# A decoder on one core: where the last norm's weights are scaled, when the low part of the summed squares is multiplied, and in which order normed blocks are read

## The chip, the core and the metric

The kernel runs on one core of a Trainium2 chip. Its engines each work off a queue of their own: TensorE (PE in the profile, its weight loads PEld), VectorE (DVE), ScalarE (ACT), GpSimd (POOL) and SyncE (SP), which here issues transfers. An instruction starts when those ahead of it on its engine have started and the semaphores that it waits for have come. The metric is the device time of one execution in microseconds (us), the median of the runs.

## What is computed

The reference is a decoder of two layers on 512 tokens of 1024 features in float32. Each layer is a half-step feed-forward block, a mixer (gated linear attention in layer 0, stick-breaking attention in layer 1) and a second half-step feed-forward block; a norm stands ahead of each, and one at the end.

```python
def rmsnorm(x, g):
    xf = x.astype(jnp.float32)
    y = xf * lax.rsqrt(jnp.mean(xf * xf, axis=-1, keepdims=True) + EPS)
    return (y * g.astype(jnp.float32)).astype(x.dtype)

def swiglu(h, w_gate, w_up, w_down):
    return (jax.nn.silu(h @ w_gate) * (h @ w_up)) @ w_down

for i in range(DEPTH):
    x = x + 0.5 * swiglu(rmsnorm(x, ffn1_norm[i]), ffn1_w_gate[i], ffn1_w_up[i], ffn1_w_down[i])
    h = rmsnorm(x, mix_norm[i])
    y = gla_mixer(h, ...) if i % N_MIXERS == 0 else sb_mixer(h, ...)
    x = x + y
    x = x + 0.5 * swiglu(rmsnorm(x, ffn2_norm[i]), ffn2_w_gate[i], ffn2_w_up[i], ffn2_w_down[i])
return rmsnorm(x, final_norm)
```

## The kernel before

**Layout.** x is kept feature by feature: eight blocks xs[k] of 128 features by 512 tokens. A product in float32 accuracy is three products of rounded parts: each matrix is split into a high part (a cast on ScalarE) and a low part (the matrix less its high part, on VectorE), and TensorE adds high by high, low by high and high by low (`mm3`). Weights are wh and wl (`Entry.parts`, cast L151, low part L152), with four buffers each. The rows of the profile name a product by its result and the two factors: ps_f<-nh,wl is a product into ps_f.

**Order of the work.** Work for TensorE stands in a list of entries (`Feed`); an entry is a stretch of weight columns with a body that yields after each quarter. Starting an entry also starts the loads and splits of the next ones. A planner then lays out each engine's queue from this program: it takes what is ready by its own estimates, and of that what comes first in the program. `tc.issue_after(ins)` adds an edge that keeps an instruction behind ins in the queue of the engine on which ins runs; `tc.high_priority` moves an instruction forward.

**A feed-forward stage** (`FFN.run`; four of them, at about 20, 553, 875 and 1430 us) goes like this. Its first entries (`feat`) multiply blocks that are not normed yet, only scaled by the gain (xh, xl), and the result is scaled by the norm's factor R afterwards; so TensorE needn't wait for the norm. `two_halves` runs the first two entries (a gate and an up column block) side by side, in halves of twelve products: gate, up, gate, up. After the third of these, in three of the stages, `sums_wide` puts in the sum over features: the squares, added up in ss by ScalarE and VectorE, are split into sh (cast, L605) and sl (low part, L607), and two products with a matrix of ones, ps_R<-sh and ps_R<-sl, give each token's sum on all partitions. Both stand behind `recent[-4]`, the fourth last product traced so far, so ahead of the last block's three products of that gate entry. `rstd_wide` makes R of it: v on VectorE (L617), logarithm, exponential and square on ScalarE (through L653), two more operations on VectorE (L624, L625).

**Normed blocks.** While entries three to six run, `normed_input` makes the normed blocks in four pieces, a pair each: piece j scales blocks j and j + 4 (xn, L878), splits both (nh L884, nl L885) and takes four differences of halves (ts, L894), from which later products are made. Entries seven and eight (numbers 6 and 7 counted from 0, still `feat`) read these blocks instead of the raw ones: `st["h"], st["l"]` are then nh and nl. All `feat` entries read the blocks in the order 0 to 7. Later column blocks (`seven`, L776) use products of halves, seven in place of eight, with weights that are sums too (s), their gates and ups in tiles o; `down` entries multiply back (ps_d, L80) and add to x: VectorE's update (L365), or for some blocks ScalarE's scaling and an adding transfer that GpSimd issues (L360, L361).

**The end.** In the last stage `to_tokens` runs between the `down` entries and the last product. It loads the final gain onto all partitions (fin, a transfer that GpSimd issues, L1636), transposes x to tokens on TensorE (L1641), copies the result on ScalarE (L1646), and scales fin on VectorE (L1649). The scaling is traced inside `tc.issue_after(copied)`, where copied is the last of the copies on ScalarE. `back_tok` does the last product by tokens (ps_bt), and `last` adds it to x (L1656), takes the final norm and sends the rows out (L1669 to L1684).

Of the kernel before, what the change touches and what calls it, by code (L numbers as in the profile page):

```python
# [21 lines left out]
KD = D // P  # L22
# [8 lines left out]
def turns(t):  # L31

    return t.rearrange("p (two n) -> p n two", two=2)


def flat(ps):

    return ps.rearrange("p (n two) -> p two n", two=2)


def pair(t):

    return t.rearrange("p (two n) -> p two n", two=2)
# [3 lines left out]
def decoder(ctx: ExitStack, tc: tile.TileContext, a: dict, out: bass.AP):  # L47
    nc = tc.nc
# [12 lines left out]
    def psum(name, tag=None):  # L61
        if tag is None:
            tag = order[turn_[0] % 8]
            turn_[0] += 1
        return pp.tile([P, T], F32, tag=tag, bufs=banks[tag], name=name)
# [9 lines left out]
    ones_r = one_r.to_broadcast([P, P])  # L75
# [3 lines left out]
    def mm(ps, l, r, first, last):  # L79
        st["pe"] = nc.tensor.matmul(ps, l, r, start=first, stop=last).ins  # L80
        recent.append(st["pe"])

    recent = []

    def mm3(ps, wh, wl, mh, ml, first, last):
        mm(ps, wh, turns(mh), first, False)
        mm(ps, wl, turns(mh), False, False)
        mm(ps, wh, turns(ml), False, last)
# [128 lines left out]
    def feat(ch, f, evac, tag=None, defer=None):  # L217


        def body(W):  # L220
            (wh, wl), = W
            ps = psum("ps_f", tag)
            for part in (range(u, u + KD // 4) for u in range(0, KD, KD // 4)):
                for k in part:
                    mm3(ps, wh[:, k], wl[:, k], st["h"][k], st["l"][k], k == 0, k == KD - 1)
                if part[-1] == KD - 1:
                    if defer is None:
                        evac(ps)
                    else:
                        defer.append((evac, ps))  # L230
                yield

        feed.q.append(Entry([(ch, lambda t: t[:, :, f * P : (f + 1) * P], KD, P)], body))
        feed.q[-1].evac = evac
# [97 lines left out]
    def down(w, r0, nf, hs, part, nxt, late=0, homes=()):  # L332


        nd = KD // nf
        src = w[r0 : r0 + nf * P, part * nd * P : (part + 1) * nd * P]
        ch = Chunk(src.rearrange("(f p) c -> p f c", p=P), nf, nd * P)
        ch.few = True

        def body(W):  # L340
            (wh, wl), = W
            acc = []

            def prod(m, fs):
                if m == len(acc):
                    acc.append(psum("ps_d"))
                s = slice(m * P, (m + 1) * P)
                for f in fs:
                    mm3(acc[m], wh[:, f, s], wl[:, f, s], hs[f][0], hs[f][1], f == 0, f == nf - 1)

            if late:
                for m in range(nd):
                    prod(m, range(nf - late))
            for m in range(nd):
                prod(m, range(nf - late if late else 0, nf))
                ps = acc[m]
                k = part * nd + m
                if m < len(homes):
                    d = sp.tile([P, T], F32, tag=homes[m], name="d")
                    nc.scalar.activation(pair(d), flat(ps), AF.Copy, scale=0.5)  # L360
                    nc.gpsimd.dma_start(xs[k], d, accum_op=ALU.add)  # L361
                    yield
                    continue
                x = pair(xs[k])
                nc.vector.scalar_tensor_tensor(  # L365
                    out=x, in0=flat(ps), scalar=0.5, in1=x, op0=ALU.mult, op1=ALU.add
                )
                if nxt is not None:
                    nxt(k)
                yield  # L370

        feed.q.append(Entry([(ch, lambda t: t, nf, nd * P)], body))
# [151 lines left out]
    st = {}  # L524
# [76 lines left out]
    def sums_wide(pool, after):  # L601

        ss = st["ss"]
        h = sp.tile([P, T], F32R, tag="sq", name="sh")
        nc.scalar.copy(h, ss)  # L605
        l = pool.tile([P, T], F32R, tag="t", name="sl")
        nc.vector.tensor_tensor(out=l, in0=ss, in1=h.bitcast(F32), op=ALU.subtract)  # L607
        st["wide"] = ps = psum("ps_R")
        with tc.high_priority(100), tc.issue_after(after):
            mm(ps, ones_r, turns(h), True, False)  # L610
            mm(ps, ones_r, turns(l), False, True)

    def rstd_wide():

        ps = st["wide"]
        v = sp.tile([P, T], F32, tag="ss", name="v")
        nc.vector.tensor_scalar(  # L617
            out=pair(v), in0=flat(ps), scalar1=1.0 / D, scalar2=EPS, op0=ALU.mult, op1=ALU.add
        )
        y = st["R"] = sp.tile([P, T], F32, tag="sq", name="R")  # L620
        act(y, v, AF.Ln)
        act(y, y, AF.Exp, scale=-0.5)
        nc.scalar.activation(ps, y, AF.Square)
        nc.vector.scalar_tensor_tensor(out=v, in0=ps, scalar=-0.5, in1=v, op0=ALU.mult, op1=ALU.mult)  # L624
        nc.vector.scalar_tensor_tensor(out=y, in0=v, scalar=1.5, in1=y, op0=ALU.add, op1=ALU.mult)  # L625

    def two_halves(between=None):

        feed.finish()
        g = [feed.start(), feed.start()]  # L630
        for i in range(3):
            for n, x in enumerate(g):
                next(x, None)
                next(x, None)
                if between is not None and (i, n) == (1, 0):
                    between(recent[-4])

    def new_norm():
        st["h"], st["l"] = st["nh"], st["nl"]

    def flush(deferred):
        for evac, ps in deferred:
# [3 lines left out]
    def exp_ln_tables(after):  # L646
        with tc.issue_after(after):
            st["tab"] = nc.scalar.preload_act_table_set("natural_log_exp_and_others").ins
# [7 lines left out]
    class FFN:  # L656
# [328 lines left out]
        def run(self, between=None):  # L985
            with tc.tile_pool(name="hp", bufs=8, reuse_waits="tile") as self.hp, tc.tile_pool(
                name="tp", bufs=5, reuse_waits="tile"
            ) as self.tp:
                st["few"] = self.hp
                new_norm()  # L990
                if st["ss"] is not None:
                    if self.after_ffn:
                        exp_ln_tables(st["closed"])
                    two_halves(lambda after: sums_wide(self.tp, after))
                    rstd_wide()
                flush(self.defer)
                def spread(todo, n):
                    for i in range(n):
                        for piece in todo[i * len(todo) // n : (i + 1) * len(todo) // n]:
                            with behind(self.last_up):  # L1000
                                piece()
                        feed.entries(1)

                spread(self.normed_input(), self.NORMED - 2)
                self.normed = True
                st["h"], st["l"] = zip(*self.n)
                todo = self.sums()
                spread(todo[:5], self.sums_by - self.NORMED)
                feed.entries(1, True)
                for piece in todo[5:]:  # L1010
                    piece()
                feed.entries(self.count - self.sums_by - 1, True)
                if between is not None:
                    with tc.issue_after(st["closed"]):
                        nc.scalar.preload_act_table_set("sqrt_and_others")
                    feed.q[feed.pos].split()
                    between(self.tp)
                feed.entries(self.total - self.count)
# [612 lines left out]
    xt = {}  # L1631

    def to_tokens(tp):
        st["tp"] = tp
        fin = st["fin"] = tp.tile([P, D], F32, tag="s", bufs=4, name="fin")
        nc.gpsimd.dma_start(fin, a["final_norm"].partition_broadcast(P))  # L1636
        for hf in range(2):
            ps = [psum("ps_T") for _ in range(NT)]
            for m in range(4):
                for i in range(NT):  # L1640
                    nc.tensor.transpose(  # L1641
                        ps[i][:, m * P : (m + 1) * P], xs[hf * 4 + m][:, i * P : (i + 1) * P], ident
                    )
            for i in range(NT):
                xt[i, hf] = xs[hf * 4 + i]
                copied = nc.scalar.copy(xt[i, hf], ps[i]).ins  # L1646

        with tc.issue_after(copied):
            nc.vector.tensor_scalar(out=fin, in0=fin, scalar1=2.0 * float(D) ** 0.5, scalar2=None, op0=ALU.mult)  # L1649

    def last(dh, i, ps, c0, c1):
# [336 lines left out]
```

## Time and profile before

| | us |
|---|---|
| median of 3 runs | 1767.38 |
| lowest, highest | 1766.87, 1767.44 |
| the profiled execution | 1767.14 |
| its span, first to last instruction | 1765.2 |
| mean granted TensorE clock | 0.999 |

The profile is of one execution. Its page gives busy times by engine. A list of waits has one line for an engine and code line and what it waited for: us in total, times, longest. A timeline row has the start, the length, the engine, the line, the operation, out<-in and the shapes, and in brackets how long the engine had idled before it and what ended that. Times are from the span's start. The ends of TensorE's products are modelled, so rows of TensorE overlap. A row of windows has the window, its length, and the busy time with the count of instructions for PE, PEld, DVE, ACT and POOL, then clock and transfer rates.

### The profile page before, as it was taken

The page shows a single profiled execution, that of the slowest core. Times are in us where ns is not written, and L with a number is a line of the kernel's source. Part 1 is how long each engine was busy: PE and PEld are TensorE (multiplying, and loading weights), DVE is VectorE, ACT ScalarE, POOL GpSimd, SP SyncE. Part 2 cuts the span into 40 slices and gives each one's busy share as a digit, 9 for nine tenths or more (in the row PEclk, how much of TensorE's full clock was granted, in tenths as well). Part 3 has the DMA queues.
Part 4 walks back from the last instruction along what each step waited for, and adds up shares of the span by engine and source line. Part 5 has one row for each costly group of instructions (what it writes and reads, how often), then busy time and mean ns, then how long its engine had stood idle before and what let it go on. Part 6 is the DMA issues. An engine that isn't in the chain of part 4 may idle for free.

```text
span 1765.2 us, 31380 instructions
## 1 busy us (share of the span) xinstructions
PE 1751.6 (99%) x12714; PEld 1630.2 (92%) x12714; DVE 1506.7 (85%) x2490; ACT 1063.3 (60%) x1899; POOL 55.7 (3%) x77
## 2 busy tenths in 40 slices
PE   9999999999999999999999999999999999999998
PEld 8999999889888899999989999999888889999997
DVE  8999797786888999889799988977898679997986
ACT  7556555554655565555656555656888745555555
POOL 0000000200000000000000000010000000000000
PEclk9999999999999999999999999999999999999999
DMA  5543435422123433444434334352212234434341
GB/s 168 155 122 106 136 105 149 113 72 72 50 89 103 125 114 120 120 120 126 133 94 132 106 123 135 102 131 83 84 49 74 70 96 132 132 99 129 110 136 61
DMA packets 186389, 193.14 MB, mean 109 GB/s; under 512 B 4931, under 2 KB 171125, under 8 KB 186245
## 3 DMA queue, kind: packets, MB, share of 16 engines
q1 hardware_dynamic: 177760, 175.91, 31.9%
q0 software_dynamic: 8240, 14.95, 4.6%
q8 instruction: 99, 1.62, 0.4%
q14 instruction: 46, 0.37, 0.1%
q10 hardware_dynamic: 244, 0.29, 0.0%
HBM read 175.17 MB, written 2.10 MB: 100 GB/s over the span
## 4 chain that ended last, share of the span: by engine, by line
PE 86%; DVE 9%; ACT 3%; issue 1%; DMA 1%; SPq 0%; DVEq 0%; ACTq 0%
PE ps_w L776 22%; PE ps_d L80 15%; PE ps_q L776 11%; PE ps_f L80 10%; PE ps_z L776 5%; PE ps_w L410 5%; PE ps_t L80 4%; PE ps_b L80 3%; PE ps_q L410 2%; DVE wl L152 1%; PE ps_z L410 1%; PE ps_z L1476 1%; PE ps_oT L1561 1%; DVE xn L878 1%; PE ps_bt L80 1%
## 5 line engine op out<-in xcount | busy, mean ns | idle before, releaser
L152 DVE TENSOR_TENSOR wl<-raw,wh 128x1024 fp32r<-128x1024 f32 x241 | 255.1, 1059 | 40.7 <-ACT wh L151 40.0
L151 ACT CAST wh<-raw 128x1024 fp32r<-128x1024 f32 x241 | 222.2, 923 | 71.5 <-PE ps_f L80 25.4
L152 DVE TENSOR_TENSOR wl<-s,wh 128x1024 fp32r<-128x1024 f32 x160 | 195.2, 1220 | 64.5 <-ACT wh L151 64.0
L776 PE MATMUL ps_w<-th,wh 128*128 128x256 f32 x864 | 239.0, 277 | 0.2
L776 PE MATMUL ps_w<-th,wl 128*128 128x256 f32 x864 | 237.7, 275 | 1.2 <-DVE wl L152 1.2
L776 PE MATMUL ps_w<-tl,wh 128*128 128x256 f32 x864 | 237.6, 275 | 0.0
L151 ACT CAST wh<-s 128x1024 fp32r<-128x1024 f32 x160 | 168.6, 1054 | 6.0 <-DVE s L762 6.0
L776 PEld LDWEIGHTS ps_w<-th,wh 128*128 128x128 f32 x864 | 165.8, 192 | 1.4 <-ACT o L813 1.1
L776 PEld LDWEIGHTS ps_w<-th,wl 128*128 128x128 f32 x864 | 165.8, 192 | 1.4 <-DVE wl L152 1.4
L80 PE MATMUL ps_f<-xh,wh 128*128 128x512 f32 x432 | 166.4, 386 | 0.0
L776 PEld LDWEIGHTS ps_w<-tl,wh 128*128 128x128 f32 x864 | 165.9, 192 | 0.0
L80 PE MATMUL ps_f<-xh,wl 128*128 128x512 f32 x432 | 164.2, 380 | 0.5 <-DVE wl L152 0.5
L80 PE MATMUL ps_f<-xl,wh 128*128 128x512 f32 x432 | 163.9, 379 | 0.0
L80 PE MATMUL ps_d<-hh,wh 128*128 128x512 f32 x416 | 157.8, 379 | 0.0
L80 PE MATMUL ps_d<-hh,wl 128*128 128x512 f32 x416 | 157.7, 379 | 0.0
L80 PE MATMUL ps_d<-hl,wh 128*128 128x512 f32 x416 | 157.7, 379 | 0.0
L152 DVE TENSOR_TENSOR wl<-rawd,wh 128x1024 fp32r<-128x1024 f32 (+1 forms) x100 | 94.8, 961 | 8.0 <-ACT wh L151 8.0
L804 ACT COPY ps_z<-ps_w 128x256 f32<-128x256 f32 x72 | 26.0, 362 | 118.1 <-PE ps_w L776 117.9
L361 POOL DMA_DIRECT2D x<-d x53 | 46.0, 913 | 1555.0 <-ACT d L360 1097.4
L80 PEld LDWEIGHTS ps_f<-xl,wh 128*128 128x128 f32 x432 | 81.7, 189 | 11.6
L80 PEld LDWEIGHTS ps_f<-xh,wl 128*128 128x128 f32 x432 | 81.7, 189 | 11.4 <-DVE wl L152 0.9
L80 PEld LDWEIGHTS ps_f<-xh,wh 128*128 128x128 f32 x432 | 81.7, 189 | 10.8
(357 smaller groups left out, 5426.0 us busy)
## 6 DMA issues: line engine op xcount, KB each, us to landing
raw<-in_ffn_w_gate_dram SPq DMA_DIRECT2D x43, 1024.0 KB, 5.4
raw<-in_ffn_w_up_dram SPq DMA_DIRECT2D x43, 1024.0 KB, 5.4
rawd<-in_ffn_w_down_dram SPq DMA_DIRECT2D x84, 512.0 KB, 3.9
x<-d POOLq DMA_DIRECT2D x53, 256.0 KB, 4.6
raw<-in_gla_w_in_dram SPq DMA_DIRECT2D x12, 1024.0 KB, 5.3
raw<-in_sb_w_in_dram SPq DMA_DIRECT2D x16, 512.0 KB, 3.7
raw<-in_gla_w_out_dram SPq DMA_DIRECT2D x4, 1024.0 KB, 5.6
raw<-in_sb_w_in_dram SPq DMA_DIRECT2D x4, 1024.0 KB, 5.1
```

The costliest lines, as they stand in the source:

```text
L80: st["pe"] = nc.tensor.matmul(ps, l, r, start=first, stop=last).ins
L151: nc.scalar.copy(h[:, k], part)
L152: nc.vector.tensor_tensor(out=l[:, k], in0=part, in1=h[:, k].bitcast(F32), op=ALU.subtract)
L361: nc.gpsimd.dma_start(xs[k], d, accum_op=ALU.add)
L410: st["pe"] = nc.tensor.matmul(ps, l_, r_, start=first and c + n == 0, stop=c == 1 and n == 2, skip_group_check=True).ins
L776: st["pe"] = nc.tensor.matmul(o, l_, r_, start=first and j + n == 0, stop=j == 3 and n == 2, skip_group_check=True).ins
L804: v["copied"] = nc.scalar.copy(z, w).ins
L878: nc.vector.scalar_tensor_tensor(out=t, in0=xs[k], scalar=g, in1=st["R"], op0=ALU.mult, op1=ALU.mult)
L1476: nc.tensor.matmul(o_, l_, r_, start=first, stop=last, skip_group_check=True)
L1561: nc.tensor.matmul(po[e * 64 : e * 64 + 64, j * P : T], self.v[j][:, c : c + 64], self.wt[p, e][bk][:, c0 : c0 + n], start=j == 0, stop=j ...
```

## The change

Three edits. `feat` reads the blocks in the order of `st["made"]`: 0 to 7 for raw blocks (set in `new_norm`), and 0, 4, 1, 5, 2, 6, 3, 7 once the blocks are normed. In `sums_wide` the product with sl stands behind `recent[-1]`, the last product traced, and no longer right behind the one with sh. The scaling of fin stands behind VectorE's last update of x (`st["updated"]`, set in `down`) instead of the last copy on ScalarE.

```diff
@@ feat
-                for k in part:
-                    mm3(ps, wh[:, k], wl[:, k], st["h"][k], st["l"][k], k == 0, k == KD - 1)
+                for i in part:
+                    k = st["made"][i]
+                    mm3(ps, wh[:, k], wl[:, k], st["h"][k], st["l"][k], i == 0, i == KD - 1)
@@ down
-                nc.vector.scalar_tensor_tensor(
+                st["updated"] = nc.vector.scalar_tensor_tensor(
                     out=x, in0=flat(ps), scalar=0.5, in1=x, op0=ALU.mult, op1=ALU.add
-                )
+                ).ins
@@ sums_wide
-        with tc.high_priority(100), tc.issue_after(after):
-            mm(ps, ones_r, turns(h), True, False)
-            mm(ps, ones_r, turns(l), False, True)
+        for r, ins, first in ((h, after[0], True), (l, after[1], False)):
+            with tc.high_priority(100), tc.issue_after(ins):
+                mm(ps, ones_r, turns(r), first, not first)
@@ two_halves
-                    between(recent[-4])
+                    between((recent[-4], recent[-1]))
@@ new_norm
-        st["h"], st["l"] = st["nh"], st["nl"]
+        st["h"], st["l"], st["made"] = st["nh"], st["nl"], range(KD)
@@ FFN.run
                 st["h"], st["l"] = zip(*self.n)
+                st["made"] = [k for j in range(4) for k in (j, j + 4)]
@@ to_tokens
-                copied = nc.scalar.copy(xt[i, hf], ps[i]).ins
-
-        with tc.issue_after(copied):
+                nc.scalar.copy(xt[i, hf], ps[i])
+
+        with tc.issue_after(st["updated"]):
             nc.vector.tensor_scalar(out=fin, in0=fin, scalar1=2.0 * float(D) ** 0.5, scalar2=None, op0=ALU.mult)
```

## The prediction

> **What bounds the kernel now.** I read the page first, then the waits of TensorE alone, then stretches of the timeline around each place that the change touches.
>
> ```profile
> span 1765.2 us, 31380 instructions
> ...
> PE 1751.6 (99%) x12714; PEld 1630.2 (92%) x12714; DVE 1506.7 (85%) x2490; ACT 1063.3 (60%) x1899; POOL 55.7 (3%) x77
> ```
>
> TensorE is busy for 99% of the span: the time is its queue of products, and only what shortens that queue, or a wait inside it, moves the end. The change removes no product, so it can win waits alone. TensorE's waits name two of them:
>
> ```profile
> PE ps_w L776 <- DVE wl L152: 1.2, 1, 1.2
> ...
> PE ps_f L80 <- DVE nl L885: 0.8, 3, 0.3
> ```
>
> These columns say too little. A product of 512 columns is drawn 0.38 long, yet in an undisturbed run the next one starts 0.22 after it (0.11 for 256 columns). So I price a wait by start to start against that spacing, and I count the product behind the wait too, which comes about 0.10 late.
>
> **First part: the last norm's weights.** These rows are of VectorE, ScalarE and TensorE near the end.
>
> ```profile
> 1713.49 0.69 DVE L1649 TENSOR_SCALAR fin<-fin 128x1024 f32<-128x1024 f32 x1 [4.02 <-DMA fin<-in_final_norm_dram]
> 1714.10 1.22 DVE L152 TENSOR_TENSOR wl<-s,wh 128x1024 fp32r<-128x1024 f32 x1
> ...
> 1735.29 1.23 DVE L152 TENSOR_TENSOR wl<-raw,wh 128x1024 fp32r<-128x1024 f32 x1 [0.30 <-ACT wh L151]
> ...
> 1740.30 0.69 DVE L1656 SCALAR_TENSOR_TENSOR x<-ps_bt,x 128x512 f32<-128x512 f32 x1 [3.78 <-PE ps_bt L80]
> ...
> 1710.38 1.05 ACT L151 CAST wh<-s 128x1024 fp32r<-128x1024 f32 x1
> ...
> 1713.82 0.28 PE L776 MATMUL ps_z<-nl,wh 128*128 128x256 f32 x1
> 1713.93 0.28 PE L776 MATMUL ps_w<-th,wh 128*128 128x256 f32 x1
> 1715.37 0.38 PE L776 MATMUL ps_w<-th,wl 128*128 128x256 f32 x1 [1.16 <-DVE wl L152]
> 1715.58 0.28 PE L776 MATMUL ps_w<-tl,wh 128*128 128x256 f32 x1
> ```
>
> The scaling of fin stands in VectorE's queue from 1709.5 (1713.49 less 4.02) and waits for its DMA. So the old edge to a copy on ScalarE holds back nothing on VectorE. Behind it is the low part of a weight (L152), whose cast was done at 1710.38 + 1.05 = 1711.43, and TensorE waits for that low part. Start to start the wait takes 1715.37 - 1713.93 - 0.11 = 1.33, and the product behind it 0.21 - 0.11 = 0.10: **1.43 in all**. Without the scaling ahead of it the low part runs from about 1711.5 to 1712.7, 1.2 before TensorE asks for it at 1713.93 + 0.11, so the whole of it is won. No DMA moves, and POOL and SP issue what they issued.
>
> The scaling's new place is behind the last update of x, just ahead of or behind the low part at 1735.29. It holds VectorE for 0.61 (1713.49 to 1714.10). Queued behind it are that low part, which belongs to the last weights of the final product, and the update at 1740.30, before which VectorE idles for 3.78; that idle time hides it. With this cover gone it would cost 0.61. The weights landed long before.
>
> **Second part: the summed squares.** Three stages begin with them; the rows are of the first, the second and the third.
>
> ```profile
> 560.06 0.48 PE L80 MATMUL ps_R<-sh,one_r 128*128 128x512 f32 x1
> 560.79 0.48 PE L80 MATMUL ps_R<-sl,one_r 128*128 128x512 f32 x1 [0.24 <-DVE sl L607]
> 561.11 0.38 PE L80 MATMUL ps_f<-xh,wh 128*128 128x512 f32 x1
> ...
> 561.54 0.38 PE L80 MATMUL ps_f<-xl,wh 128*128 128x512 f32 x1
> ...
> 561.31 0.69 DVE L617 TENSOR_SCALAR v<-ps_R 128x512 f32<-128x512 f32 x1 [0.57 <-PE ps_R L80]
> ...
> 561.95 1.05 ACT L151 CAST wh<-raw 128x1024 fp32r<-128x1024 f32 x1 [1.94 <-PE ps_f L80]
> 562.90 0.63 ACT L653 ACTIVATE R<-v 128x512 f32<-128x512 f32 x1
> ...
> 882.51 0.38 PE L80 MATMUL ps_R<-sh,one_r 128*128 128x512 f32 x1
> ...
> 882.94 0.38 PE L80 MATMUL ps_f<-xh,wh 128*128 128x512 f32 x1
> ...
> 883.79 1.05 ACT L151 CAST wh<-raw 128x1024 fp32r<-128x1024 f32 x1 [2.41 <-PE ps_f L80]
> 884.74 0.62 ACT L653 ACTIVATE R<-v 128x512 f32<-128x512 f32 x1
> ...
> 1437.73 0.38 PE L80 MATMUL ps_R<-sh,one_r 128*128 128x512 f32 x1
> ...
> 1438.55 0.38 PE L80 MATMUL ps_f<-xh,wh 128*128 128x512 f32 x1
> ```
>
> In the first, the two products of the sums take 561.11 - 560.06 = 1.05. The first of them was late itself, so the product behind it keeps its 0.32; with the low part no longer waited for the two take 0.32 + 0.22 = 0.54: **0.51 won**. Moved behind three products it starts near 561.04, after the 560.79 at which its input was there. In the third, 0.82 becomes 0.44: **0.38**. In the second, 882.94 - 882.51 = 0.43 shows no wait: nothing.
>
> What is late next? VectorE's v (L617) waits for the low part, ScalarE's logarithm (L653) for v, and all normed blocks for that. But the logarithm also stands behind the weight cast, which waits for the three products that now come earlier. In the first stage their last one moves from 561.54 to 560.82, so cast and logarithm move from 561.95 and 562.90 to 561.23 and 562.18; v, from 561.45 to 562.14, is just in time. VectorE's chain is then 0.72 earlier. In the second the cast comes at 883.57 and the logarithm at 884.52: 0.22 earlier.
>
> **Third part: the order of the normed blocks.** Rows of the fifth to eighth product entry of a stage, then of the very first stage.
>
> ```profile
> 587.24 0.38 PE L80 MATMUL ps_f<-nh,wl 128*128 128x512 f32 x1
> 587.87 0.48 PE L80 MATMUL ps_f<-nl,wh 128*128 128x512 f32 x1 [0.25 <-DVE nl L885]
> 588.19 0.38 PE L80 MATMUL ps_f<-nh,wh 128*128 128x512 f32 x1
> ...
> 588.41 0.68 DVE L885 TENSOR_TENSOR nl<-xn,nh 128x512 fp32r<-128x512 f32 x1
> ...
> 589.35 1.22 DVE L152 TENSOR_TENSOR wl<-raw,wh 128x1024 fp32r<-128x1024 f32 x1
> ...
> 591.00 0.38 PE L80 MATMUL ps_f<-nh,wl 128*128 128x512 f32 x1
> ...
> 911.18 1.22 DVE L152 TENSOR_TENSOR wl<-raw,wh 128x1024 fp32r<-128x1024 f32 x1
> ...
> 912.84 0.38 PE L80 MATMUL ps_f<-nh,wl 128*128 128x512 f32 x1
> ...
> 44.81 0.90 PE L80 MATMUL ps_f<-nh,wh 128*128 128x512 f32 x2
> ...
> 45.76 0.38 PE L80 MATMUL ps_d<-hh,wh 128*128 128x512 f32 x1
> ...
> 46.49 0.38 PE L80 MATMUL ps_f<-nh,wh 128*128 128x512 f32 x1
> ...
> 47.65 1.22 DVE L152 TENSOR_TENSOR wl<-raw,wh 128x1024 fp32r<-128x1024 f32 x1
> 49.08 0.38 PE L80 MATMUL ps_f<-nh,wl 128*128 128x512 f32 x1
> ...
> 24.10:48.80 24.70, 24.12 (x108) 19.87 (x108) 24.70 (x44) 15.64 (x25) 0.00 (x0) 1.00 0.17 53
> ```
>
> Blocks are made in pairs 0 and 4, 1 and 5, 2 and 6, 3 and 7, and read from 0 to 7; block 3, of the last pair, is read fourth and waited for. That is 587.87 - 587.24 - 0.22 = 0.41, and 0.10 behind it: 0.51, in three stages (the waits list counts three): **1.53**. In the new order it is read seventh, nine products or 1.9 later. The last block's low part ends at 588.41 + 0.68 = 589.09 and is read two products ahead of 591.00, less what TensorE has won (1.02): 589.5, in time.
>
> The wait that could take its place is the next entry's weight: its low part ends at 589.35 + 1.22 = 590.57, is seen about 0.06 later, and is wanted at 591.00. TensorE will be there 0.51 + 0.51 = 1.02 sooner (589.98), the weight 0.72 sooner (589.91): just in time by 0.07. In the second stage 912.84 - 0.51 = 912.33 stands against 911.18 + 1.22 + 0.06 - 0.22 = 912.24. I take no cost; the bound on the other side, with VectorE not earlier at all, is 0.65 + 0.10, 0.13 + 0.10, and for the third (0.89 won there against the same 0.37 to spare) 0.52 + 0.10: 1.6.
>
> In the first stage the same waits cost 0.90 - 0.60 = 0.30 and 46.49 - 45.76 - 0.43 = 0.30. There VectorE is busy for all of 24.70 us before 48.80 (third time of the last row) and has no reason to be earlier. Its next low part ends at 47.65 + 1.22 = 48.87, and TensorE takes it at 49.08, so TensorE would now wait there for what it has won. I take 0; the bounds are 0.60 won and 0.15 lost (a new wait's 0.10 and rounding).
>
> **Sum.** 1.43 + 0.51 + 0.38 + 1.53 = 3.85 us. The profiled execution took 1767.14 with a span of 1765.2, and becomes 1763.3; it lies 0.24 under the median of the runs, so for the median 1767.38 - 3.85 = **1763.5**.
>
> The Trainium skill, TensorE: Matmul & The Clock Gate, section Single matmul latency, gives a lone warm matmul (398 + N) / 2.4 ns, 379 for 512 columns, while a stream is spaced by about 216: a wait then costs its idle time and 163 ns, and nothing is said of the product behind. The rows have the 0.38 and the 0.22. By the page the 0.10 behind each of six waits would not be there to win, and the sum would be about 3.25.
>
> **Rivals.**
> - *VectorE doesn't come earlier*, and the next weight's low part takes the place of the wait for block 3 in all three stages: 1763.5 + 1.6 = 1765.1. For it: the 0.07 to spare. Against it: the cast's release, worked out above.
> - *The first stage keeps what it wins*: 1763.5 - 0.6 = 1762.9. For it: the program that orders the queues may place other products in the gap, as it did with the ps_d at 45.76. Against it: VectorE's full queue.
> - *The 0.10 behind the waits isn't won*: 1763.5 + 0.6 = 1764.1. Against it: every wait above shows it. The page named above would give this.
> - *The first part doesn't do what it says*: the planner puts another wait into that place, and TensorE's 1.43 stays: 1764.9. Against it: nothing else stands in VectorE's idle 4.02.
> - *Slower*: one low part of a weight falls back in VectorE's queue. The planner orders by its own estimates, and these move. If the split at 589.35 falls behind two other splits (1.22 each) and a low part of a block (0.68), TensorE waits 3.12 - 0.07 + 0.10 = 3.15 in each of the three stages, 9.45 in all: 1773.0. It decides from 1.3 a stage on, where it eats the 3.85. Against it: in that stretch VectorE works off its queue in the order of the program, which the change leaves.
>
> **Chances.** The sum as it stands 0.57 (its own range 1763.0 to 1763.8); the first stage keeps its gain 0.13; VectorE not earlier 0.14; the 0.10 stays 0.04; the first part fails 0.05; slower 0.07. About 0.2% (3.5 us, to 1763.85) is what a measurement can tell from no change; so faster is 0.57 + 0.13 = 0.70, within it 0.14 + 0.04 + 0.05 = 0.23, slower 0.07. The sum lies only 0.3 beyond that bound. The range goes from 1762.9 less 0.6 (the spread of the runs) to 1763.5 + 1.6 + 1.43, two rivals at once: 1762.3 to 1766.5, with only the slower case outside.
>
> **What would show it.** Right: no wait for fin on VectorE, its scaling near 1734; no wait for sl; no wait for nl; starts 0.22 apart from 587 to 590. Wrong: a wait of TensorE for wl at the eighth entry, near 590, 912 or 1467, of more than 0.1; a wait in the first stage near 48 that is much shorter or longer than 0.5; VectorE's logarithm chain not earlier; or a different order on VectorE between 565 and 596. The forecast as a whole fails if new waits of 3 us or more appear in stages that the change doesn't touch.

## The result, and the profile after

The changed kernel takes 1763.96 us in the median of 17 runs (1763.23 to 1765.51), the kernel before 1767.44 in 17 runs beside it (1766.87 to 1769.01). The ratio is 0.9979 with a 95% interval of 0.9972 to 0.9985: 3.48 us, or 0.2%, are won. The prediction was 1763.5, a sum of 3.85 us. The interval of the ratio, 2.65 to 4.95 us, holds that too; what is missing of it is read from the traces.

First the head of the page after, then a line of the list of TensorE's waits:

```profile
span 1762.0 us, 31383 instructions
...
PE 1750.1 (99%) x12714; PEld 1630.7 (93%) x12714; DVE 1506.8 (86%) x2490; ACT 1064.1 (60%) x1899; POOL 55.6 (3%) x77
```

```profile
PE ps_f L80 <- DVE wl L152: 1.0, 2, 0.5
```

The engines' counts are those of before: only waits went. The list no longer has a line for nl, for sl or for the 1.2 of ps_w. In its place the one line on ps_f and wl has grown: before it counted one wait of 0.5, now two. The new one stands in the first stage, below. (Code lines are one or two higher than before.)

**The end.** Timeline of the changed kernel, VectorE and then TensorE:

```profile
1709.67 1.23 DVE L152 TENSOR_TENSOR wl<-s,wh 128x1024 fp32r<-128x1024 f32 x1 [2.00 <-ACT wh L151]
...
1731.69 0.68 DVE L1651 TENSOR_SCALAR fin<-fin 128x1024 f32<-128x1024 f32 x1
...
1737.08 0.69 DVE L1658 SCALAR_TENSOR_TENSOR x<-ps_bt,x 128x512 f32<-128x512 f32 x1 [3.57 <-PE ps_bt L80]
...
1712.14 0.28 PE L777 MATMUL ps_w<-th,wh 128*128 128x256 f32 x1
1712.25 0.28 PE L777 MATMUL ps_w<-th,wl 128*128 128x256 f32 x1
1712.36 0.28 PE L777 MATMUL ps_w<-tl,wh 128*128 128x256 f32 x1
```

The low part now waits for its own cast only, ends at 1709.67 + 1.23 = 1710.90, and TensorE reads it 1.35 later. The three products start 0.11 apart, where 1.33 and 0.10 were lost. The scaling of fin runs at 1731.69, and VectorE still idles for 3.57 (3.78 before) ahead of its next update.

**The sums.** The first of the three stages, a weight load (PEld), TensorE and ScalarE, and behind them the product with sh and the logarithm of the second:

```profile
560.27 0.18 PEld L80 LDWEIGHTS ps_R<-sh,one_r 128*128 128x128 f32 x1
...
560.39 0.38 PE L80 MATMUL ps_R<-sh,one_r 128*128 128x512 f32 x1
560.61 0.38 PE L80 MATMUL ps_f<-xh,wh 128*128 128x512 f32 x1
...
561.04 0.38 PE L80 MATMUL ps_f<-xl,wh 128*128 128x512 f32 x1
561.25 0.38 PE L80 MATMUL ps_R<-sl,one_r 128*128 128x512 f32 x1
...
562.46 0.64 ACT L654 ACTIVATE R<-v 128x512 f32<-128x512 f32 x1
...
881.80 0.38 PE L80 MATMUL ps_R<-sh,one_r 128*128 128x512 f32 x1
...
883.86 0.64 ACT L654 ACTIVATE R<-v 128x512 f32<-128x512 f32 x1
```

Both products of the sums stand in the stream at its spacing, and so do those of the other two stages. Even the product with sh, 0.13 late before, is on time here, though its load came only 0.12 ahead of it; the last section returns to that. From the product with sh to the logarithm it is 562.46 - 560.39 = 2.07, and was 562.90 - 560.06 = 2.84: 0.77 shorter. In the second stage it is 2.06 against 884.74 - 882.51 = 2.23: 0.17 shorter.

**The normed blocks.** The same stage up to its eighth entry, VectorE, weight loads and TensorE, then the same two products in the two stages that follow:

```profile
588.91 1.22 DVE L152 TENSOR_TENSOR wl<-raw,wh 128x1024 fp32r<-128x1024 f32 x1
...
589.75 0.19 PEld L80 LDWEIGHTS ps_f<-nh,wh 128*128 128x128 f32 x1
590.18 0.19 PEld L80 LDWEIGHTS ps_f<-nh,wl 128*128 128x128 f32 x1 [0.25 <-DVE wl L152]
...
589.96 0.38 PE L80 MATMUL ps_f<-nh,wh 128*128 128x512 f32 x1
590.18 0.48 PE L80 MATMUL ps_f<-nh,wl 128*128 128x512 f32 x1
590.50 0.38 PE L80 MATMUL ps_f<-nl,wh 128*128 128x512 f32 x1
...
911.60 0.48 PE L80 MATMUL ps_f<-nh,wl 128*128 128x512 f32 x1
911.91 0.38 PE L80 MATMUL ps_f<-nl,wh 128*128 128x512 f32 x1
...
1466.46 0.48 PE L80 MATMUL ps_f<-nh,wl 128*128 128x512 f32 x1
1466.78 0.38 PE L80 MATMUL ps_f<-nl,wh 128*128 128x512 f32 x1
```

No product waits for nl. But look at the loads. The one at 589.75 belongs to the product at 589.96: in the stream a load stands one product ahead of the product that uses it. The low part of the weight ends at 588.91 + 1.22 = 590.13, and its load comes at 590.18, together with its product and not ahead of it. That product isn't late (590.18 - 589.96 = 0.22); it is only drawn 0.48 long. The next one is late: 590.50 - 590.18 - 0.22 = 0.10. The same 0.10 stands at 1466.78 and, with its rounding, at 911.91.

**The first stage**, VectorE and TensorE:

```profile
47.89 1.22 DVE L152 TENSOR_TENSOR wl<-raw,wh 128x1024 fp32r<-128x1024 f32 x1
...
43.55 0.38 PE L80 MATMUL ps_f<-nl,wh 128*128 128x512 f32 x1
...
48.30 0.38 PE L80 MATMUL ps_f<-nh,wh 128*128 128x512 f32 x1
49.16 0.48 PE L80 MATMUL ps_f<-nh,wl 128*128 128x512 f32 x1 [0.49 <-DVE wl L152]
49.48 0.38 PE L80 MATMUL ps_f<-nl,wh 128*128 128x512 f32 x1
...
86.03 0.38 PE L777 MATMUL ps_w<-th,wh 128*128 128x256 f32 x1
```

A wait of 49.16 - 48.30 - 0.22 = 0.64, and 0.10 behind it, have taken the place of two waits of 0.30: about 0.15 lost.

### The profile page after: what moved, and what is told of

Same layout as the page of the kernel before. It is cut to its first block, busy times and chain, and to the rows that moved or that the text cites. A ratio compares the mean times of both kernels' runs of the same rounds, so it can differ in the third digit from the quotient of the medians.

```text
span 1762.0 us, 31383 instructions
## 1 busy us (share of the span) xinstructions
PE 1750.1 (99%) x12714; PEld 1630.7 (93%) x12714; DVE 1506.8 (86%) x2490; ACT 1064.1 (60%) x1899; POOL 55.6 (3%) x77
## 4 chain that ended last, share of the span: by engine, by line
PE 88%; DVE 7%; ACT 3%; issue 1%; DMA 1%; SPq 0%; DVEq 0%; ACTq 0%
PE ps_w L777 20%; PE ps_d L80 15%; PE ps_f L80 14%; PE ps_q L777 10%; PE ps_z L777 5%; PE ps_w L411 5%; PE ps_t L80 4%; PE ps_b L80 4%; PE ps_q L411 2%; DVE wl L152 2%; PE ps_z L1478 1%; PE ps_z L411 1%; PE ps_oT L1563 1%; PE ps_bt L80 1%; PE ps_T L1548 1%
```

## The experiments

The theory after these readings: the waits are won as they were priced, and the eighth entry's weight takes back 0.10 in each of three stages and 0.15 in the first. The rivals: a part doesn't work by itself for the reason given, or the losses are chance of one execution. Effects of 0.1 to 0.5 us are below the spread of the runs, so they are read from start to start in the traces, with the medians beside them.

### Each part alone

The kernel before, with the new edge for fin alone:

```diff
-                nc.vector.scalar_tensor_tensor(
+                st["updated"] = nc.vector.scalar_tensor_tensor(
...
-        with tc.issue_after(copied):
+        with tc.issue_after(st["updated"]):
...
```

> Only the scaling of fin is put behind VectorE's last update of x; the rest is the kernel before. Theory: VectorE's queue alone made TensorE wait near 1714, and the 1.33 and the 0.10 behind it go: 1.43 us less, about 1766.0 against 1767.4. No other wait changes. Rival: the low part at 1714.10 would have waited for something else, or the scaling is in the way near 1734; then less than 0.5 is won, and TensorE shows a new wait between 1712 and 1745.

The kernel before, with the old edge and the scaling on ScalarE:

```diff
-            nc.vector.tensor_scalar(out=fin, in0=fin, scalar1=2.0 * float(D) ** 0.5, scalar2=None, op0=ALU.mult)
+            nc.scalar.activation(fin, fin, AF.Copy, scale=2.0 * float(D) ** 0.5)
```

> The kernel before, with the scaling of fin done by ScalarE behind its last copy, where the edge of before now binds, and not by VectorE. Theory: the cause was VectorE's queue in order, in which the scaling waited for its transfer; without the scaling there the low part runs near 1711.5 and the same 1.43 us is won: about 1766.0. ScalarE does the scaling near 1736 to 1740, where it has time. Rival: it is the transfer of fin itself, or another instruction in the stretch from 1709.5, that delays VectorE or TensorE there; then the wait near 1714 stays and the time is 1767.4.

Against 1766.97 for the kernel before, the first took 1765.54 (ratio 0.9992, 0.9983 to 1.0001) and the second 1765.59 (0.9992, 0.9983 to 1.0001): 1.43 and 1.38 less. The intervals reach 1, so the traces decide. In the first the low part runs at 1711.52, and the three products at 1713.99, 1714.10 and 1714.22 start 0.11 apart. The second, VectorE and TensorE (ScalarE scales fin at 1739.04):

```profile
1712.56 1.23 DVE L152 TENSOR_TENSOR wl<-s,wh 128x1024 fp32r<-128x1024 f32 x1 [2.00 <-ACT wh L151]
...
1715.14 0.28 PE L776 MATMUL ps_w<-th,wl 128*128 128x256 f32 x1
1715.25 0.28 PE L776 MATMUL ps_w<-tl,wh 128*128 128x256 f32 x1
```

The transfer of fin is the same (7.26 from issue to landing, 7.14 before) and the wait is gone, since nothing on VectorE stands behind the transfer any more. VectorE's queue was the cause; a place outside that queue serves as well as one late in it.

The sums alone, and the order alone, each in the kernel before:

```diff
-        with tc.high_priority(100), tc.issue_after(after):
-            mm(ps, ones_r, turns(h), True, False)
-            mm(ps, ones_r, turns(l), False, True)
+        for r, ins, first in ((h, after[0], True), (l, after[1], False)):
+            with tc.high_priority(100), tc.issue_after(ins):
+                mm(ps, ones_r, turns(r), first, not first)
...
```

> Only the product with sl stands three products later; the rest is the kernel before. Theory: 0.51 is won at 560 and 0.38 at 1438, nothing at 882; the median falls by about 0.9 to 1766.5, and the waits for nl and the wait before fin's low part stay as long as before. ScalarE's cast and logarithm come 0.7 earlier after 560. Rival: the wait only moves, because the chain behind the sums (v, logarithm, normed blocks) is unchanged in time, so that the wait for nl near 588 grows by what was won at 560; then the products near 591 stand as late as before.

```diff
+                st["made"] = [k for j in range(4) for k in (j, j + 4)]
...
-                for k in part:
+                for i in part:
+                    k = st["made"][i]
...
```

> Only the order in which normed blocks are read is changed. Theory: the three waits for nl of 0.51 go, but the eighth entry's weight, without the 0.72 and 0.22 that the earlier sums bring, is then late by about 0.14 in each of the three later stages, and 0.10 is lost behind it: 0.27 us won in each. In the first stage 0.2 to 0.3 is lost. Together 0.5 to 0.6 us, about 1766.9. Rival: the weight does not hang on the sums' chain; then each stage keeps 0.41, and with the loss in the first 1.0 us is won: 1766.4.

With the sums alone the median is 1766.10 (0.9993, 0.9984 to 1.0002): 0.87 less, about the number expected, but not by that road alone. TensorE at the wait for nl and late in the last stage, and VectorE there:

```profile
586.32 0.38 PE L80 MATMUL ps_f<-nh,wl 128*128 128x512 f32 x1
586.80 0.48 PE L80 MATMUL ps_f<-nl,wh 128*128 128x512 f32 x1
...
1494.43 0.38 PE L776 MATMUL ps_w<-th,wh 128*128 128x256 f32 x1 [0.35 <-ACT ps_z L804]
...
1490.81 0.69 DVE L761 TENSOR_TENSOR s<-raw 128x512 f32<-128x512 f32 x1 [1.32 <-DMA raw<-in_ffn_w_gate_dram]
```

The waits at the sums are gone. The wait for nl neither stays, as the theory had it, nor grows, as the rival had it: it falls from 0.41 to 586.80 - 586.32 - 0.22 = 0.26, since VectorE's chain came earlier by more than TensorE did (587.87 - 586.80 = 1.07 against 587.24 - 586.32 = 0.92). And this execution has a wait of 1.32 on VectorE for a transfer of weights, which reaches TensorE through ScalarE (0.35 idle at 1494.43). From there to 1505 TensorE loses some 1.25 of what it had won. The load of that weight landed 8.78 after its issue here. It took 7.17 in the profile of before and 6.98 in that of the changed kernel, where VectorE does not wait for it; in the first repeat of the changed kernel, below, it took 8.04 and VectorE waited again (0.57). I take it for chance of an execution. So this median is more than one term.

With the order alone the median is 1766.31 (0.9994, 0.9985 to 1.0003): 0.66 less. VectorE and TensorE at the eighth entry:

```profile
589.67 1.21 DVE L152 TENSOR_TENSOR wl<-raw,wh 128x1024 fp32r<-128x1024 f32 x1
...
590.56 0.38 PE L80 MATMUL ps_f<-nh,wh 128*128 128x512 f32 x1
590.93 0.48 PE L80 MATMUL ps_f<-nh,wl 128*128 128x512 f32 x1
591.25 0.38 PE L80 MATMUL ps_f<-nl,wh 128*128 128x512 f32 x1
```

Here the product itself is late, by 590.93 - 590.56 - 0.22 = 0.15, and the next by 0.10: 0.25 of the 0.51 is given back, as the theory had it, and as much in the two stages that follow. So the weight does hang on the sums' chain, and in the changed kernel the sums' part is worth 0.15 more in this stage than what it wins at the sums themselves.

### The weight that is late next

Three kernels beside a repeat of the changed one: the old order in the first stage; the low part of the eighth entry's weight ahead of the differences of halves that remain; both, with the first stage left as it was before. `self.first` marks the first stage:

```diff
                 st["h"], st["l"] = zip(*self.n)
-                st["made"] = [k for j in range(4) for k in (j, j + 4)]
+                if not self.first:
+                    st["made"] = [k for j in range(4) for k in (j, j + 4)]
```

> The changed kernel with the order 0 to 7 kept in the first feed-forward stage. Theory: in that stage the new order only moves the wait from nh and nl to the eighth entry's weight (0.65 and 0.10 at 49.2), and 0.15 to 0.3 is lost by it; with the old order the two waits of 0.30 come back, the one at 49.2 goes, and TensorE is 0.15 to 0.3 earlier by 50 us against the changed kernel. The later stages stay. Rival: the loss came from the opening and not from the order; then TensorE stands at the same place after 50 us, less what it already differed at 43 us.

In piece j of `normed_input`, with `st["low"]` the last nl on VectorE:

```diff
+                if j == 3:
+                    with tc.issue_after(st["low"]):
+                        feed.q[feed.pos + 2].split()
                 ts = self.tp.tile([P, 4, H], F32, tag="s", bufs=4, name="ts")
                 sub(ts[:, 0], x[:, H:T], x[:, 0:H])
```

> The changed kernel, in which the low part of the eighth entry's weight comes right behind the last nl on VectorE, ahead of the differences (ts) that are left: three of them in the first stage, one in the others. Theory: the weight is what TensorE is late by now. In the first stage it comes 1.0 earlier and the wait of 0.75 goes; in the other three it comes 0.34 earlier and the 0.10 behind it goes. Together 1.05 us less than the changed kernel. Rival: VectorE is the bound in these stretches, and what is moved back makes TensorE wait as long at the next weight or for th and tl; then new waits of 0.3 to 1.0 show within 10 us, and the median is that of the changed kernel.

Both edits, the second with `j == 3 and not self.first`:

> Both together for the first stage undone: the changed kernel with the old order in the first stage and the weight's low part behind the last nl in the three later stages alone. Theory: the first stage is as with the old order (0.15 to 0.3 better than the changed kernel), the later three win 0.10 each: 0.45 to 0.6 less than the changed kernel, but 0.4 to 0.6 more than with the weight moved in all four stages. Rival: as above, what is moved back is wanted just as early, and the later stages win nothing.

The changed kernel again, beside them:

> The changed kernel once more, beside the next three on the same chip. Theory: the opening of the stream, before the first stage, differs by some 0.2 us from one execution to the next, and so does the wait for sh at 560; the median is 1763.5 to 1764.0 when the kernel before has 1767.0 to 1767.4, and the last 0.10 behind the eighth entry's weight shows in the three later stages again. Rival: that 0.10 was chance in one profile; then it is missing in one of the three stages at least.

These last three kernels were run a second time:

> The changed kernel a third time, as the measure for the next two. The median is 1763.8 to 1764.0 where the kernel before has 1767.4; the profile shows either opening, 1.5 us apart.

> The kernel with the old order in the first stage and the eighth entry's weight behind the last nl in the later three, again. Theory: it is 0.3 to 0.6 us under the changed kernel, 1763.3 to 1763.6, and no product behind that weight is late in the later stages. Rival: the earlier median of 1763.55 was chance, and the two agree within 0.1.

> The kernel with the weight moved in all four stages, again. Theory: the first stage wins 0.75 at 50 us and gives 0.5 of it back by 88, where TensorE waits for ps_z; with the three later 0.10 the median is 0.4 to 0.6 under the changed kernel, 1763.3 to 1763.5. Rival: the waits near 71, 80 and 88 were chance of one execution; then they are missing in this profile and the gain is 1.0.

| kernel | median us (runs), first time | second time | ratio to before, 95% |
|---|---|---|---|
| the changed kernel, repeated | 1763.85 (11) | 1763.85 (11) | 0.9980 (0.9971 to 0.9989), both times |
| weight earlier, four stages | 1763.24 (11) | 1763.13 (9) | 0.9977 (0.9968 to 0.9986), 0.9976 (0.9967 to 0.9986) |
| weight earlier in three, old order in the first | 1763.55 (9) | 1763.46 (11) | 0.9977 (0.9968 to 0.9987), 0.9977 (0.9968 to 0.9986) |
| old order in the first | 1764.94 (11) | | 0.9983 (0.9974 to 0.9992) |

The kernel before took 1767.53 and 1767.58 beside them. Both kernels with the weight moved are below the changed one, both times, by 0.3 to 0.7, but the intervals overlap; their gain rests on the traces. In both repeats the products behind the weight were late again at the three places, so that is no chance of one profile.

The second run with the weight moved in three stages, VectorE and TensorE at the eighth entry:

```profile
588.05 1.24 DVE L152 TENSOR_TENSOR wl<-raw,wh 128x1024 fp32r<-128x1024 f32 x1
...
589.46 0.38 PE L80 MATMUL ps_f<-nh,wh 128*128 128x512 f32 x1
589.67 0.38 PE L80 MATMUL ps_f<-nh,wl 128*128 128x512 f32 x1
589.89 0.38 PE L80 MATMUL ps_f<-nl,wh 128*128 128x512 f32 x1
```

The low part ends at 589.29, ahead of the load (589.46); the product is drawn 0.38 long again, and the next stands 0.22 behind it. The 0.10 is won, and it was lateness of a load, not of a product.

The old order in the first stage, VectorE and TensorE:

```profile
49.30 1.24 DVE L152 TENSOR_TENSOR wl<-raw,wh 128x1024 fp32r<-128x1024 f32 x1
...
44.98 0.38 PE L80 MATMUL ps_f<-nl,wh 128*128 128x512 f32 x1
...
50.76 0.38 PE L80 MATMUL ps_f<-nh,wl 128*128 128x512 f32 x1
```

These are the same places in TensorE's queue as 43.55 and 49.48 of the changed kernel: 5.78 against 5.93, so the new order costs 0.15 in this stage. The median, expected 0.15 to 0.3 below the repeat, lies 1.1 above it, but says nothing on the order, since the runs fall into two groups (five at 1763.46 to 1763.78, six at 1764.94 to 1766.88). The profiled run, at 1766.04, is of the second: its opening is 1.4 longer than in the first profile of the changed kernel, and it loses 1.0 where VectorE waits 0.98 for the weights near 1491.

With the weight moved in the first stage too, the second run, TensorE:

```profile
43.23 0.38 PE L80 MATMUL ps_f<-nl,wh 128*128 128x512 f32 x1
...
48.41 0.38 PE L80 MATMUL ps_f<-nl,wh 128*128 128x512 f32 x1
...
85.00 0.28 PE L777 MATMUL ps_q<-tl,wh 128*128 128x256 f32 x1
85.45 0.38 PE L777 MATMUL ps_w<-th,wh 128*128 128x256 f32 x1 [0.18 <-ACT ps_z L805]
```

The three products at 43.23, 48.41 and 85.45 are those at 43.55, 49.48 and 86.03 of the changed kernel. To the second it is 5.18 against 5.93: the whole 0.75 is won. From there to the third it is 37.04 against 36.55: 0.49 of it is given back, 85.45 - 85.00 - 0.11 = 0.34 of that in a wait for ScalarE's copy into ps_z. Both runs of this kernel show it. VectorE is busy for all of the 25.59 from 48.41 to 74.00, and at the end of that its product o (73.83, read next by ScalarE) is only 0.47 earlier than in the changed kernel (74.29), where TensorE was 1.07 earlier at 48.41; 0.32 of either is the opening. So here, where VectorE has no idle time, what is drawn forward for one wait is missing at another. The way from there to the copy at 85 is not shown; VectorE itself idles for 1.41 before 76.26. Still, of the versions that ran this one and the one with the old first stage are the best; which of the two is better, the runs don't tell.

## Why the prediction was right, and where it was off

| term | predicted | shown |
|---|---|---|
| fin | 1.43 | both gaps gone, as in the two kernels that change this alone |
| sums, first, second, third stage | 0.51, 0, 0.38 | won: all products of the sums at the stream's spacing |
| waits for nl, three stages | 1.53 | gone in all three |
| the weight that is wanted next | 0 | -0.10 in each of three stages, -0.30 |
| first stage | 0 | -0.15 |
| sum | 3.85 | 3.40 |

The medians can't tell 3.40 from 3.85. The interval of the 3.48 goes from 2.65 to 4.95, and the two repeats gave 3.68 and 3.73; that 0.45 is missing rests on the traces. So there is luck in how near the number came. The median lies 0.16 above the sum's own range (1763.0 to 1763.8) and nearer to the rival whose 0.10 isn't won (1764.1) than to the sum, and only the traces rule that rival out. The 3.5 us that the prediction took for the least that a measurement can tell from no change were too many: the interval is 1.15 wide to either side.

The spans of the two profiles differ by 3.2. TensorE's opening is 0.23 longer in the one after, the product with sh is no longer late (0.13, and 0.10 behind it), which the prediction had left as it was, and some 0.2 is lost in steps of 0.10 at places that the change doesn't touch.

**Fin.** Right in place and size. The low part ran earlier than forecast (1709.67 and not 1711.5), as VectorE and TensorE were both ahead by then; it has 1.35 to spare. The prediction said 1.2, but its own figures give 1713.93 + 0.11 - 1712.7 = 1.34.

**The sums, and what hangs on them.** The waits are won as priced. That the logarithm comes earlier, because the cast ahead of it waits for three products that move forward, is borne out: counted from the product with sh it is 0.77 and 0.17, where 0.72 and 0.22 were forecast. The kernel with the order alone shows what it was worth: without the earlier sums the product with the eighth entry's weight is 0.15 late and the next one 0.10. That is the rival "VectorE doesn't come earlier", at the price worked out for the second stage (0.13 + 0.10), since TensorE is only 0.51 sooner there too.

**The weight that is wanted next: a step that failed.** The prediction had TensorE there at 589.98 and the weight, seen 0.06 after its end, at 589.91, "just in time by 0.07", and took no cost. Two things were wrong. The weight was held against the start of its product, but it is the load that needs it, and the load stands 0.21 ahead. By the rows of the last section the product behind a late load starts 0.32 after that load, so even the 0.07 would have cost some 0.32 - 0.07 - 0.22 = 0.03 in each stage (an estimate). And the 0.07 weren't there: the load came at 590.18 together with the product, and so it did in the two stages that follow, which costs the full 0.10. Why the 0.07 shrank to nothing, the runs don't show. The kernel with this low part earlier shows that nothing else is in the 0.10: with the load ahead again, it is won.

**The first stage.** "TensorE would now wait there for what it has won" holds: the low part is not earlier. It ends 5.56 behind the first of the two places compared above in both kernels (47.89 + 1.22 - 43.55, and 49.30 + 1.24 - 44.98 with the old order). The value taken was 0, and it was the bound of 0.15, but with a term that the prediction left out. With the old order a product ps_d stands in the gap (45.76 before); with the new one nothing is put there, and that product, 0.22, has yet to come (54.23). The first product with the low part is 0.17 earlier (49.16 - 43.55 against 50.76 - 44.98), and the one behind it is 0.10 late: 0.22 - 0.17 + 0.10 = 0.15. Against the rival that this stage keeps what it wins stand these rows, and the kernel that drew the weight forward there and gave 0.49 of 0.75 back.

**The other rivals.** The 0.10 behind a wait is real: in the kernel with fin alone the product behind the one that had waited starts 0.11 after it and not 0.21. The Trainium skill, TensorE: Matmul & The Clock Gate, section Single matmul latency, gives a lone warm product of 512 columns 379 ns, and nothing on the next one. The rows draw a product in the stream 0.38 long and one whose load came with it 0.48. Slower didn't come: on VectorE the only changes of order between 565 and 596 are that in one piece two nl now stand together (575.42), with a difference of halves behind them, and nothing waits for either.

## What to carry to other kernels

Hold a just-in-time operand against the load of the stationary matrix, not against its product. Here the load stands 0.21 us ahead; one that came 0.12 ahead cost nothing, and those that came with their product made the next one 0.10 late. A scaling that waited for a transfer held up all that stood behind it on VectorE, though its edge named an instruction of ScalarE; move such an instruction to where its result is wanted, or to an engine that idles. A product that fills a wait has to run all the same: when the wait goes, count it. Before a wait is counted as won, name the next operand on the same engine and its slack; where that engine has none, the win comes back as the next wait, with its own restart.

## What the runs showed of the hardware

**A load that comes late.** How late the load of sh comes in the first of the three stages differs from one execution to the next. Four executions of kernels with the new sums give a scale; in brackets is the distance from the column before.

| execution | load of sh | its product | the next product |
|---|---|---|---|
| the changed kernel | 560.27 | 560.39 (0.12) | 560.61 (0.22) |
| its second repeat | 560.27 | 560.35 (0.08) | 560.59 (0.24) |
| its first repeat | 561.94 | 561.97 (0.03) | 562.26 (0.29) |
| weight earlier in four stages, first time | 561.72 | 561.73 (0.01) | 562.04 (0.31) |

In the last three the next product starts 0.31 to 0.32 after the load; in the first it stands at the stream's 0.22. So a load that was late by some 0.09 of its 0.21 cost nothing here, and the later ones cost the more, the later they came, up to the 0.10 of a load that comes with its product.

**The opening.** TensorE's opening differs from one execution of the same kernel to the next, by more than most terms of this study. The changed kernel and its first repeat, a row of the windows each, and three products of the repeat's timeline:

```profile
8.00:12.00 4.00, 4.00 (x27) 3.46 (x27) 3.51 (x8) 3.94 (x11) 0.00 (x0) 1.00 1.13 329
```

```profile
8.00:12.00 4.00, 4.00 (x18) 3.39 (x18) 2.78 (x7) 2.39 (x6) 0.00 (x0) 1.00 1.14 329
```

```profile
8.28 0.63 PE L1781 MATMUL ps_f<-xh,wh 128*128 128x512 f32 x1
8.71 0.63 PE L1781 MATMUL ps_f<-xh,wl 128*128 128x512 f32 x1
...
45.25 0.38 PE L80 MATMUL ps_f<-nl,wh 128*128 128x512 f32 x1
```

In the same 4 us TensorE counts 27 instructions in the one and 18 in the other, where products still start 0.43 apart, twice the 0.22 of later; the granted clock is given as 1.00 in both. The product at 45.25 is that at 43.55 of the first profile: 1.70 later, in the same kernel. The Trainium skill, TensorE: Matmul & The Clock Gate, section Part 1: The HAM clock gate, says that TensorE begins at half its clock, that the window after which it is raised runs freely, and so that the number of slow products changes from run to run; its 426.7 and 215.7 ns between starts of 512 columns agree with the 0.43 and 0.22. That the clock is the cause was not tried here. For the reader it means that two spans of one execution each can't be compared to better than some 1.7 us, and that small effects are to be read between two places of the same stretch.
